# Feed-forward by seven block products, the gated rows through DRAM, the second product as a phase of its own

## The chip, the core and the metric

The kernel runs on one NeuronCore of a Trainium2 chip. The core has a matrix engine (TensorE, "PE" in the rows; its weight loads are "PEld"), a vector engine (VectorE, "DVE"), a scalar engine (ScalarE, "ACT"), GpSimd ("POOL") and SyncE ("SP"), which here issues all DMAs. Each engine works through its own instructions in order; semaphores join them. Operands lie in SBUF (128 partitions); matmuls write to PSUM, eight banks of 128 x 512 float32. The metric is the device time of one execution, in microseconds.

## The reference

Three layers on 1024 tokens of width 1024 (an attention layer with a window, a gated linear attention layer, and a layer with three mixers), with 16 meta tokens ahead of the tokens in the third. The change touches only the feed-forward of that third layer, at the end of the program:

```python
f = causal_dwconv(rms_norm_2(h, norm_ffn_pre) @ ffn_up, ffn_conv)   # 1024 -> 2*2816, 3 taps over tokens
gate, val = jnp.split(f, 2, axis=-1)
f = (jax.nn.gelu(gate, approximate=True) * val) @ ffn_down          # 2816 -> 1024
h = h + rms_norm_2(f, norm_ffn_post)
return h[:, N_META:]
```

Everything is float32. A product of two float32 matrices is made from three matmuls in the type float32r: each operand is split into a high part (a copy in float32r) and a low part (the rest), and high x high, high x low and low x high are summed in PSUM.

## The kernel before

The program is written in a framework that allocates buffers by name ("tag") from pools with a stated number of copies ("bufs"), sets the semaphores itself, and fixes each engine's order of instructions beforehand from a timeline of its own. The order written in the source gives the priority; what is planned as ready earlier can be put ahead. All instructions of the program stand in one straight line, without loops at run time.

`out_proj2` goes through the nine token tiles (16 meta tokens, then 8 x 128). For each it makes the output projection, adds it to the residual, stores the row to DRAM (`hd`), and calls `norm_T` (L290), which normalises the row, transposes it on TensorE in two halves and writes high and low parts of the transposed tokens to `hT3h` and `hT3l` (128 x 8 k x 1040). The caller's `ahead` (L1789) loads and splits the first weights during tiles 3 and 4.

`ffn` goes through 22 blocks of 128 gate and 128 value columns. `block(j)` loads the block's weights of both products and splits them: `wload` (L108) with a copy on ScalarE (L103) and a subtraction on VectorE (L106), four pieces for `ffn_up` ("whi", "wlo"), two for `ffn_down` ("dnh", "dnl"). `up` makes the first product for the two parts in three pieces of 342 tokens each, 24 matmuls a piece (L132 to L134), copies each out of PSUM (L1642), applies the convolution (one scaling on ScalarE, L1644, two multiply-adds on VectorE, L1646), the GELU (L1649) and the gate product (L1650), and splits the gated rows ("fh", "fl"). After every second block `down` makes the second product of the pair for 8 token tiles in two halves of 512 columns, 6 matmuls each, and adds it to an accumulator in SBUF (`acc`, L1662). The first product uses PSUM groups A and E (three banks), the second group B (two banks). In the last pair, `final` closes each token tile: sum of squares (L1670), the post-gain on GpSimd (L1675; VectorE for the last tile), scaling and residual on VectorE (L1676), the store (L1677).

GpSimd has no work in this stage but that of `final` and the reciprocal roots (L97).

## Time and profile before

| | |
|---|---|
| median of 3 runs | 3154.92 us (3152.09 to 3157.61) |
| profiled execution | 3161.62 us, of which the span from first to last instruction is 3159.8 us |
| mean granted TensorE clock | 0.983 of full |
| TensorE busy | 3041.3 us (96%) |
| VectorE, ScalarE, GpSimd busy | 1851.5 (59%), 1400.4 (44%), 463.9 us (15%) |
| feed-forward, first to last matmul | 2395.4 to 3149.4 us |

The rows that follow come from the profile of that one execution. A group row gives the line, engine, operation, the tiles written and read, the shape, the count, then the busy time in us and the mean duration of one in ns, then idle time of the engine ahead of these instructions and what ended it. A row of the timeline gives the start and the duration in us; "x2" joins instructions in a row. Matmuls are pipelined: their recorded durations overlap, so that the distance from start to start says what one costs.

### The profile page before, as it was taken

What the parts mean: (1) busy time and instruction counts of PE and PEld (TensorE: products, weight loads), DVE (VectorE), ACT (ScalarE), POOL (GpSimd) and SP (SyncE); (2) the same over time, 40 slices, a digit from 0 to 9 for tenths busy, and PEclk for the clock granted to TensorE, in tenths of its full rate; (3) what the DMA queues carried; (4) which work ended last, traced back from release to release, by engine and by line L of the source; (5) the groups of instructions that cost most, each with busy time, mean ns of one, the idle gap of its engine ahead of it and who ended that gap; (6) DMA issues with size and microseconds to landing.
All of it is one profiled execution on the core that took longest, in us unless ns stands there. A gap on an engine that the chain in (4) does not pass through costs nothing.

```text
span 3159.8 us, 52021 instructions
## 1 busy us (share of the span) xinstructions
PE 3041.3 (96%) x19891; PEld 2771.9 (88%) x19891; DVE 1851.5 (59%) x4811; ACT 1400.4 (44%) x3415; POOL 463.9 (15%) x506
## 2 busy tenths in 40 slices
PE   8899999999999999998999999899999999999997
PEld 5799999889888789998789999788889999999996
DVE  5667757777766765446547434666555345454446
ACT  4689845555553643323236222345534423233323
POOL 2467621332220000000000000201000000000003
PEclk9999999999999999999999999898999999999999
DMA  5222210110042231113321121313132111111113
GB/s 213 71 75 90 86 40 6 33 34 6 15 144 101 101 101 58 57 39 99 120 77 50 57 70 48 85 46 94 48 123 93 43 40 50 45 47 57 44 40 117
DMA packets 140329, 218.21 MB, mean 69 GB/s; under 512 B 24408, under 2 KB 80784, under 8 KB 140080
## 3 DMA queue, kind: packets, MB, share of 16 engines
q1 hardware_dynamic: 140080, 214.90, 21.6%
q8 instruction: 156, 2.56, 0.3%
q14 instruction: 93, 0.76, 0.1%
HBM read 171.87 MB, written 42.97 MB: 68 GB/s over the span
## 4 chain that ended last, share of the span: by engine, by line
PE 83%; DVE 7%; DMA 4%; ACT 3%; issue 2%; POOL 1%; SPq 0%; DVEq 0%; POOLq 0%; ACTq 0%
PE mm L132 17%; PE mm L133 17%; PE mm L134 17%; PE te L405 3%; PE po L1534 3%; PE sc L391 3%; PE sc L132 2%; PE sc L134 2%; PE sc L133 2%; PE po L661 2%; PE po L612 2%; DMA woraw<-in_w_out 1%; ACT EB L646 1%; PE sc L882 1%; PE tp L255 1%
## 5 line engine op out<-in xcount | busy, mean ns | idle before, releaser
L132 PE MATMUL mm<-whi,hT 128*128 128x256 f32 (+1 forms) x1760 | 513.6, 292 | 19.1 <-DVE gsl L828 4.8
L133 PE MATMUL mm<-wlo,hT 128*128 128x256 f32 (+1 forms) x1760 | 507.2, 289 | 3.5 <-POOL wlo L106 3.5
L132 PEld LDWEIGHTS mm<-whi,hT 128*128 128x128 f32 x1760 | 337.0, 192 | 26.6 <-DVE gsl L828 6.2
L133 PEld LDWEIGHTS mm<-wlo,hT 128*128 128x128 f32 x1760 | 337.5, 192 | 7.3 <-POOL wlo L106 4.8
L132 PE MATMUL mm<-hT3h,whi 128*128 128x342 f32 (+3 forms) x1020 | 325.9, 320 | 0.0
L133 PE MATMUL mm<-hT3l,whi 128*128 128x342 f32 (+3 forms) x1020 | 325.2, 319 | 0.0
L134 PE MATMUL mm<-hT3h,wlo 128*128 128x342 f32 (+3 forms) x1020 | 324.7, 318 | 0.0
L134 PE MATMUL mm<-whi,lo 128*128 128x256 f32 x1040 | 300.7, 290 | 0.9 <-POOL lo L106 0.8
L103 ACT CAST whi<-wraw 128x512 fp32r<-128x512 f32 (+2 forms) x205 | 135.7, 677 | 211.3 <-PE mm L133 79.1
L132 PE MATMUL mm<-hT,whi 128*128 128x352 f32 (+3 forms) x640 | 219.8, 344 | 3.6 <-ACT a L1018 1.8
L1662 DVE TENSOR_TENSOR acc<-acc,sc 128x512 f32<-128x512 f32 x160 | 108.7, 685 | 192.8 <-PE sc L134 192.0
L133 PE MATMUL mm<-hT,whi 128*128 128x352 f32 (+3 forms) x640 | 218.2, 341 | 0.1
L134 PE MATMUL mm<-hT,wlo 128*128 128x352 f32 (+3 forms) x640 | 217.9, 342 | 0.0
L106 DVE TENSOR_TENSOR wlo<-wraw,whi 128x512 fp32r<-128x512 f32 (+1 forms) x161 | 125.9, 789 | 154.1 <-ACT whi L103 153.2
L407 ACT COPY wT<-te 128x512 f32<-128x512 f32 (+2 forms) x368 | 159.3, 453 | 124.1 <-PE te L405 115.8
L134 PE MATMUL mm<-whi,hT 128*128 128x256 f32 (+3 forms) x720 | 205.3, 285 | 0.0
L134 PEld LDWEIGHTS mm<-whi,lo 128*128 128x128 f32 x1040 | 201.8, 194 | 3.1 <-POOL lo L106 1.6
L133 PEld LDWEIGHTS mm<-hT3l,whi 128*128 128x128 f32 x1020 | 192.0, 188 | 6.3
L132 PEld LDWEIGHTS mm<-hT3h,whi 128*128 128x128 f32 x1020 | 191.8, 188 | 6.0
L134 PEld LDWEIGHTS mm<-hT3h,wlo 128*128 128x128 f32 x1020 | 191.9, 188 | 3.6
L97 POOL TENSOR_TENSOR c<-c,cm 128x2 f32<-128x2 f32 (+1 forms) x170 | 126.1, 743 | 404.0 <-DVE c L95 358.1
L97 POOL TENSOR_TENSOR inv<-inv,cm 128x1 f32<-128x1 f32 (+1 forms) x87 | 52.5, 604 | 891.7 <-DVE inv L95 891.7
(490 smaller groups left out, 7687.9 us busy)
## 6 DMA issues: line engine op xcount, KB each, us to landing
adraw<-in_adaln_w SPq DMA_DIRECT2D x48, 512.0 KB, 3.9
wraw<-in_ffn_up SPq DMA_DIRECT2D x85, 256.0 KB, 2.8
wraw<-in_w_ab SPq DMA_DIRECT2D x26, 512.0 KB, 3.8
woraw<-in_w_out SPq DMA_DIRECT2D x48, 256.0 KB, 3.0
wraw<-in_w_gla SPq DMA_DIRECT2D x48, 256.0 KB, 2.9
wraw<-in_w_in SPq DMA_DIRECT2D x24, 512.0 KB, 4.3
dnraw<-in_ffn_down SPq DMA_DIRECT2D x44, 256.0 KB, 2.5
fraw<-qkd SPq DMA_DIRECT2D x32, 260.0 KB, 4.2
```

Source lines behind the costliest of these rows:

```text
L97: nc.gpsimd.tensor_tensor(out, out, self.cm05[:p, :n], op=ALU.pow)
L103: nc.scalar.copy(hi, src)
L106: (lo_eng or nc.vector).tensor_tensor(lo, src, hi.bitcast(F32), op=ALU.subtract)
L132: mmul(ps, ah, bh, start=k == 0, stop=False)
L133: mmul(ps, ah, bl, start=False, stop=False)
L134: mmul(ps, al, bh, start=False, stop=k == nk - 1)
L391: self.nc.tensor.matmul(sp, q[x][:, m], keys, start=x == 0, stop=last and x == 1)
L405: nc.tensor.transpose(ps[:n, j * 128:j * 128 + nq], E, self.ident[:nq, :nq])
L407: nc.scalar.copy(w[:n, :m, :nq], ps.rearrange("p (j t) -> p j t", j=4)[:n, :m, :nq])
L612: nc.tensor.matmul(ops[:, m * 64:m * 64 + 64], w[:, 2 * x + m, :], v[:, i], start=x0 + x + m == 0, stop=x0 + x == len(kt) - 1, skip_group_ ...
L1534: nc.tensor.matmul(ops[:n, :64], w[:kn, y, :n], v[:kn, x, r], start=x == 0, stop=x == i)
L1662: nc.vector.tensor_tensor(acc[:, t, sl], acc[:, t, sl], ps, op=ALU.add)
```

## The change

The matrices of the first product are taken as 2 x 2 blocks: the weights of block j by two halves of the 1024 inner rows and by gate and value columns, the tokens by the same two inner halves and by two halves of the 1024 tokens (514 wide, with two tokens ahead for the convolution). Eight block products give the four results; the change makes them from seven products of sums and differences of blocks (`SEVEN`: weight block, sign, other weight block, token block, sign, other token block).

- `out_proj2` writes the normalised, transposed tokens unsplit into `hf` (128 x 8 x 1026 float32), and splits at once only the two quarters that appear alone in a product (`quads`).
- `tok_op` makes the five other token operands in the first block, when they are first asked for, in two slices of 258 and 256 tokens each (4 x 258 elements a partition) through one buffer `tsum`; products 4 and 6 are summed on GpSimd, 2, 3 and 5 on VectorE; each slice is then split. After block 0 `hf` is freed.
- For each block, `up_raw` loads the weights as two tiles of 512 KB. For each product, `up_op` makes the two half operands (128 x 256): a sum or difference on GpSimd into `uptmp` where there is a sign (five of seven products), then the split. Two pools hold the results, 2 and 9 buffers of each part, and one `uptmp` each.
- For each product and each of two column pieces, 12 matmuls of 258 columns go to one of eight PSUM banks in turn. The first three products are copied to SBUF by ScalarE; VectorE adds the other four out of PSUM, and GpSimd makes the four combinations that lie in SBUF, for each column piece.
- `gate` does convolution, GELU and gate product for a column piece of 256 tokens, gate and value parts as before, and stores the gated rows to DRAM (`fd`, 256 KB).
- The second product follows when all 22 blocks are done (two steps are loaded ahead during block 20): for each half of the tokens and each of the 22 blocks, `step` loads gated rows (256 KB) and `ffn_down` rows (2 x 256 KB), splits them, and 24 matmuls of 512 columns add into all eight banks, which hold the half's result over all 22 blocks. The last three blocks go tile by tile, and `final` works out of the banks, with the post-gain on VectorE.

```diff
@@ out_proj2
-                self.norm_T(h[:n], n, G, None, hT[0], hT[1], c0)
+                xs, m = self.norm_rows(h[:n], n), min(n, 2) if t < 0 else n
                 for half in range(2):
+                    k0, c = 4 * half, max(c0 - 14, 0)
+                    pv = self.half_T(xs, n, half, self.tp).rearrange("p (j t) -> p j t", j=4)[:, :, n - m:n]
+                    dst = hf[:, k0:k0 + 4, c:c + m]
+                    nc.vector.tensor_tensor(dst, pv, G[:, k0:k0 + 4].unsqueeze(2).to_broadcast([128, 4, m]), op=ALU.mult)
+                    x0, x1 = max(c, 512 * half), min(c + m, 514 + 512 * half)
+                    if x0 < x1:
+                        q = slice(x0 - 512 * half, x1 - 512 * half)
+                        self.split(*(z[:, :, q] for z in quads[half]), hf[:, k0:k0 + 4, x0:x1],
+                                   "dve" if half == 0 else "act")
@@ ffn, with the functions removed (they stand above) left out
+    SEVEN = [((1, 0), 1, (1, 1), (0, 0), 0, None),
+             ((0, 0), 1, (0, 1), (1, 1), 0, None),
+             ((0, 0), 1, (1, 1), (0, 0), 1, (1, 1)),
+             ((1, 1), 0, None, (1, 0), -1, (0, 0)),
+             ((0, 0), 0, None, (0, 1), -1, (1, 1)),
+             ((1, 0), -1, (0, 0), (0, 0), 1, (0, 1)),
+             ((0, 1), -1, (1, 1), (1, 0), 1, (1, 1))]
+    def up_raw(self, j, pool):
+        raws = []
+        for q in range(2):
+            raw = pool.tile([128, 2, 2, 256], F32, tag="upraw", name="upraw", bufs=2)
+            self.nc.sync.dma_start(raw, self.I["ffn_up"][j].rearrange("p (h q i) c -> q p h i c", h=2, q=2)[q])
+            raws.append(raw)
+        return raws
+    def up_op(self, raws, i, pools):
+        nc = self.nc
+        (r, h), sign, other = self.SEVEN[i][:3]
+        parts = []
+        for raw in raws:
+            pool, bufs = next(pools)
+            src = raw[:, h, :, 128 * r:128 * r + 128]
+            if sign:
+                r2, h2 = other
+                tmp = pool.tile([128, 2, 128], F32, tag="uptmp", name="uptmp", bufs=1)
+                nc.gpsimd.tensor_tensor(tmp, src, raw[:, h2, :, 128 * r2:128 * r2 + 128],
+                                        op=ALU.add if sign > 0 else ALU.subtract)
+                src = tmp
+            p = [pool.tile([128, 2, 128], F32R, tag="up" + z, name="up" + z, bufs=bufs) for z in "hl"]
+            self.split(*p, src)
+            parts.append(p)
+        return lambda k: tuple(z[:, k % 2] for z in parts[k // 2])
+    def ffn(self, hd, hf, close_hf, quads, wp, early, out):
+        nc, I = self.nc, self.I
+        st = ExitStack()
+        sp = st.enter_context(self.pool("hS", 1))
+        w1 = st.enter_context(self.pool("wtsu", 1))
+        p = st.enter_context(self.pool("ffn", 2))
+        cw = p.tile([128, 3, 44], F32, name="ffnc", bufs=1)
+        nc.sync.dma_start(cw, I["ffn_conv"])
+        fd = [self.dp.tile([128, 2, 512], F32, name=f"fd{j}") for j in range(22)]
+        self.psum(mm="ABDCABDE")
+        pools = itertools.cycle([(wp, 2)] + [(w1, 9)] * 4 + [(wp, 2)] + [(w1, 9)] * 5)
+        halves = [slice(0, 512), slice(512, 1024)]
+        sums = {}
+        def tok_op(i):
+            qa, sign, qb = self.SEVEN[i][3:]
+            if not sign:
+                return quads[qa[0]]
+            if i not in sums:
+                a, b = (hf[:, 4 * r:4 * r + 4, 512 * h:512 * h + 514] for r, h in (qa, qb))
+                op = [sp.tile([128, 4, 514], F32R, name=f"s{i}{z}") for z in "hl"]
+                for c in (slice(0, 258), slice(258, 514)):
+                    s = (slice(None), slice(None), c)
+                    t = sp.tile([128, 4, 258], F32, tag="tsum", name="tsum")[:, :, :c.stop - c.start]
+                    (nc.gpsimd if i in (4, 6) else nc.vector).tensor_tensor(
+                        t, a[s], b[s], op=ALU.add if sign > 0 else ALU.subtract)
+                    self.split(op[0][s], op[1][s], t)
+                sums[i] = op
+            return sums[i]
+        def block(j, raws, first):
+            x = [[p.tile([128, 2, 258], F32, tag=f"fx{part}", name="fx") for part in range(2)] for c in range(2)]
+            s = [[None] * 7 for c in range(2)]
+            for i in range(7):
+                w = first if first and i == 0 else self.up_op(raws, i, pools)
+                op = tok_op(i)
+                for c in range(2):
+                    ps = self.mm()[:, :258]
+                    for k in range(4):
+                        wh, wl = w(k)
+                        th, tl = (z[:, k, 256 * c:256 * c + 258] for z in op)
+                        nc.tensor.matmul(ps, wh, th, start=k == 0, stop=False)
+                        nc.tensor.matmul(ps, wh, tl, start=False, stop=False)
+                        nc.tensor.matmul(ps, wl, th, start=False, stop=k == 3)
+                    g, u = x[c]
+                    if i < 3:
+                        s[c][i] = p.tile([128, 258], F32, tag=f"fs{i}", name=f"fs{i}")
+                        nc.scalar.copy(s[c][i], ps)
+                    s0, s1, s2 = s[c][:3]
+                    if i == 2:
+                        nc.gpsimd.tensor_tensor(s2, s2, s0, op=ALU.subtract)
+                        nc.gpsimd.tensor_tensor(s2, s2, s1, op=ALU.subtract)
+                    elif i == 3:
+                        nc.vector.tensor_tensor(u[:, 0], ps, s0, op=ALU.add)
+                        nc.gpsimd.tensor_tensor(s0, s2, u[:, 0], op=ALU.add)
+                    elif i == 4:
+                        nc.vector.tensor_tensor(g[:, 1], ps, s1, op=ALU.add)
+                        nc.gpsimd.tensor_tensor(s1, s2, g[:, 1], op=ALU.add)
+                    elif i == 5:
+                        nc.vector.tensor_tensor(u[:, 1], ps, s1, op=ALU.add)
+                    elif i == 6:
+                        nc.vector.tensor_tensor(g[:, 0], ps, s0, op=ALU.add)
+                        self.gate(p, cw, j, x[c], fd[j][:, :, 256 * c:256 * c + 256])
+        def step(h, k):
+            pool, n = ((P, 2), (P, 2), (Q, 4), (Q, 4), (Q, 4), (Q, 4))[(22 * h + k) % 6] if h + k > 1 else (P, 2)
+            fr = pool.tile([128, 512], F32, tag="fr", name="fr", bufs=2)
+            nc.sync.dma_start(fr, fd[k][:, h])
+            f = [pool.tile([128, 512], F32R, tag="f" + z, name="f" + z, bufs=n) for z in "hl"]
+            self.split(*f, fr)
+            d = [pool.tile([128, 1024], F32R, tag="dn" + z, name="dn" + z, bufs=n) for z in "hl"]
+            for sl in halves:
+                raw = pool.tile([128, 512], F32, tag="dnraw", name="dnraw", bufs=2)
+                nc.sync.dma_start(raw, I["ffn_down"][k][:, sl])
+                self.split(*(z[:, sl] for z in d), raw)
+            return f, d
+        with ExitStack() as s2:
+            for j in range(22):
+                if j:
+                    raws, w0 = self.up_raw(j, wp), None
+                block(j, raws, w0)
+                if j == 0:
+                    close_hf()
+                    P = s2.enter_context(self.pool("dn1", 1, side="right"))
+                if j == 20:
+                    ready = [step(0, 0), step(0, 1)]
+            st.close()
+            Q = s2.enter_context(self.pool("dn2", 1))
+            post = Q.tile([128, 1024], F32, name="npost2")
+            nc.sync.dma_start(post, I["norm_ffn_post"].partition_broadcast(128))
+            self.psum(dn="AABBCDDE")
+            LAST = 3
...
+            for h in range(2):
+                banks = [[self.bank("dn") for i in range(2)] for t in range(4)]
+                def mm(t, i, k, f, d):
+                    a, b = ([z[:, s] for z in q] for q, s in ((f, slice(128 * t, 128 * t + 128)), (d, halves[i])))
+                    for n, (e, g) in enumerate(((0, 0), (0, 1), (1, 0))):
+                        nc.tensor.matmul(banks[t][i], a[e], b[g], start=k == 0 and n == 0, stop=k == 21 and n == 2)
+                for k in range(22 - LAST):
+                    f, d = ready.pop(0) if ready else step(h, k)
+                    for t in range(4):
+                        for i in range(2):
+                            mm(t, i, k, f, d)
+                last = [step(h, k) for k in range(22 - LAST, 22)]
+                for t in range(4):
+                    for i in range(2):
+                        for k in range(LAST):
+                            mm(t, i, 22 - LAST + k, *last[k])
+                    final(4 * h + t, banks[t])
+    def gate(self, p, cw, j, x, dst):
+        nc = self.nc
+        ys = []
+        for part in range(2):
+            y = p.tile([128, 2, 256], F32, tag=f"fy{part}", name="fy")
+            c = 22 * part + j
+            nc.scalar.activation(y, x[part][:, :, 2:258], AF.Copy, scale=cw[:, 2, c:c + 1])
+            for tap in range(2):
+                nc.vector.scalar_tensor_tensor(y, x[part][:, :, tap:tap + 256], cw[:, tap, c:c + 1], y, op0=ALU.mult,
+                                               op1=ALU.add)
+            ys.append(y)
+        g, u = ys
+        nc.scalar.activation(g, g, AF.Gelu_apprx_tanh)
+        nc.vector.tensor_tensor(g, g, u, op=ALU.mult)
+        nc.sync.dma_start(dst, g)
```

## Rows read from the trace of the kernel before

**Rows 1.** The page's part 4: who holds the chain that ended last.
```profile
PE 83%; DVE 7%; DMA 4%; ACT 3%; issue 2%; POOL 1%; SPq 0%; DVEq 0%; POOLq 0%; ACTq 0%
```

**Rows 2.** Three stretches: us, busy PE, PEld, DVE, ACT, POOL, clock, DMA.
```profile
2395.40:2450.00 54.60, 53.31 (x341) 52.53 (x340) 32.85 (x42) 28.59 (x47) 1.41 (x2) 1.00 0.33 108
2450.00:3095.00 645.00, 645.00 (x3656) 602.59 (x3655) 304.99 (x363) 203.67 (x316) 0.00 (x0) 1.00 0.15 46
3095.00:3149.60 54.60, 48.64 (x246) 39.97 (x244) 39.91 (x66) 20.79 (x50) 22.03 (x20) 0.97 0.36 121
```

**Rows 3.** Timeline, TensorE: first and last of 31, 32, 12 matmuls.
```profile
2449.79 0.32 PE L132 MATMUL mm<-hT3h,whi 128*128 128x342 f32 x1
...
2454.48 0.32 PE L132 MATMUL mm<-hT3h,whi 128*128 128x342 f32 x1
...
1299.72 0.28 PE L132 MATMUL mm<-whi,hT 128*128 128x256 f32 x1
...
1303.44 0.28 PE L133 MATMUL mm<-wlo,hT 128*128 128x256 f32 x1
...
2460.39 0.39 PE L132 MATMUL sc<-dnh,fh 128*128 128x512 f32 x1
...
2462.95 0.39 PE L134 MATMUL sc<-dnh,fl 128*128 128x512 f32 x1
```

**Rows 4.** VectorE: two groups by shape, then three rows of its timeline.
```profile
L106 DVE TENSOR_TENSOR qTl<-tp,qTh 128x256 fp32r<-128x256 f32 x80 | 33.5, 419 | 12.9 <-ACT qTh L103 12.0
L106 DVE TENSOR_TENSOR wlo<-wraw,whi 128x1024 fp32r<-128x1024 f32 x26 | 32.9, 1266 | 41.8 <-ACT whi L103 41.7
...
3096.32 0.75 DVE L1646 SCALAR_TENSOR_TENSOR fy<-fx,ffnc,fy 128x510 f32<-128x510 f32 x1 [2.31 <-ACT fy L1644]
...
3108.15 0.69 DVE L1650 TENSOR_TENSOR fy<-fy 128x510 f32<-128x510 f32 x1
...
3110.82 1.28 DVE L106 TENSOR_TENSOR dnl<-dnraw,dnh 128x512 fp32r<-128x512 f32 x2
```

**Rows 5.** ScalarE, groups by shape: a cast, a scaling, a wide cast.
```profile
L103 ACT CAST fh<-fy 128x256 fp32r<-128x256 f32 x1 | 0.4, 391 | 0.0
L1644 ACT ACTIVATE fy<-fx,ffnc 128x510 f32<-128x510 f32 x2 | 1.4, 724 | 0.1
L103 ACT CAST whi<-wraw 128x1024 fp32r<-128x1024 f32 x26 | 27.2, 1046 | 73.7 <-PE mm L133 36.3 <-DMA wraw<-in_w_in 20.4 <-DMA wraw<-in_w_ab 14.9
```

**Rows 6.** GpSimd, groups by shape: sums over SBUF in an earlier layer.
```profile
L182 POOL TENSOR_TENSOR adacc<-adacc,adpr 128x512 f32<-128x512 f32 x84 | 107.9, 1285 | 37.4 <-ACT adpr L179 25.9 <-ACT adacc L179 6.8 <-PE sc L391 1.9
L182 POOL TENSOR_TENSOR adacc<-adacc,adpr 128x256 f32<-128x256 f32 x28 | 20.7, 740 | 10.6 <-ACT adpr L179 6.7 <-ACT adacc L179 2.5
```

**Rows 7.** One VectorE line (durations min/median/max), then two pairs beside GpSimd.
```profile
L365 DVE TENSOR_TENSOR qn<-jk,jk x64: 404/424/1524, 72.1 to 878.0; 128x256 f32<-128x256 f32 x64
...
210.89 2.65 POOL L182 TENSOR_TENSOR adacc<-adacc,adpr 128x512 f32<-128x512 f32 x2 [0.47 <-ACT adpr L179]
...
212.36 1.47 DVE L365 TENSOR_TENSOR qn<-jk,jk 128x256 f32<-128x256 f32 x1
...
3133.05 2.96 POOL L1675 TENSOR_TENSOR acc<-acc,npost 128x512 f32<-128x512 f32 x2
...
3133.11 3.45 DVE L1676 SCALAR_TENSOR_TENSOR acc<-acc,inv,h 128x512 f32<-128x512 f32 x2
```

**Rows 8.** Timeline: last output-projection matmul, and the last token tile's low part.
```profile
2394.82 0.39 PE L134 MATMUL mm<-wo 128*128 128x512 f32 x1
...
2408.69 0.69 DVE L106 TENSOR_TENSOR hT3l<-xt,hT3h 128x512 fp32r<-128x512 f32 x1
```

**Rows 9.** Timeline: the last matmul, and VectorE's last two instructions.
```profile
3149.00 0.40 PE L134 MATMUL sc<-dnh,fl 128*128 128x512 f32 x1
...
3155.40 1.41 DVE L1676 SCALAR_TENSOR_TENSOR acc<-acc,inv,h 128x512 f32<-128x512 f32 x2 [0.73 <-POOL inv L97]
```

**Rows 10.** DMA issues: times, KB each, median us from issue to landing.
```profile
adraw<-in_adaln_w SPq DMA_DIRECT2D x48, 512.0 KB, 3.9
```

More of the change, by code (lines that the diff above doesn't have):

```diff
@@ new lines, in ffn, with final @@
+    def ffn(self, hd, hf, close_hf, quads, wp, early, out):
[59 more added lines that the diff above has]
+                        self.gate(p, cw, j, x[c], fd[j][:, :, 256 * c:256 * c + 256])
+        raws, w0 = early
+        P = None
+        steps = []
+        def step(h, k):
[26 more added lines that the diff above has]
+            LAST = 3
+            def final(t, banks):
+                h = Q.tile([128, 1024], F32, tag="h", name="h", bufs=2)
@@ L1666, in final @@
                 nc.sync.dma_start(h, hd[t + 1])
+                y = Q.tile([128, 1024], F32, tag="y", name="y", bufs=2)
                 ss, rs = self.sums()
@@ L1669, in final @@
                 for i, sl in enumerate(halves):
-                    nc.scalar.activation(self.te(), acc[:, t, sl], AF.Square, accum_out=ss[:, i:i + 1])
+                    jk = Q.tile([128, 512], F32, tag="jk", name="jk", bufs=2)
+                    nc.scalar.activation(jk, banks[i], AF.Square, accum_out=ss[:, i:i + 1])
+                    nc.vector.tensor_tensor(y[:, sl], banks[i], post[:, sl], op=ALU.mult)
                 nc.vector.tensor_tensor(rs, ss[:, 0:1], ss[:, 1:2], op=ALU.add)
@@ L1673, in final @@
                 for i, sl in enumerate(halves):
-                    y = acc[:, t, sl]
-                    (nc.gpsimd if t < 7 else nc.vector).tensor_tensor(y, y, post[i], op=ALU.mult)
-                    nc.vector.scalar_tensor_tensor(y, y, rs, h[:, sl], op0=ALU.mult, op1=ALU.add)
-                    nc.sync.dma_start(out[t * 128:t * 128 + 128, sl], y)
-            for g in range(10):
-                Bs = []
-                for j in (2 * g, 2 * g + 1):
-                    Bs.append(block(j))
-                    up(Bs[-1], FC)
-                for t in range(8):
-                    down(Bs, t, g == 0)
@@ L1687, in ffn @@
-            Bs = [block(20)]
-            up(Bs[0], FC)
-            Bs.append(block(21))
-            post = []
-            for sl in halves:
-                post.append(self.wp.tile([128, 512], F32, tag="wraw", name="npost2", bufs=RAWS))
-                nc.sync.dma_start(post[-1], I["norm_ffn_post"][sl].partition_broadcast(128))
-            FC = [(14, 512), (526, 258), (784, 256)]
-            up(Bs[1], FC[:1])
-            up(Bs[1], FC[1:2])
-            for ts, nxt in ((range(0, 3), FC[2:]), (range(3, 6), None), (range(6, 8), None)):
-                for t in ts:
-                    down(Bs, t, False)
-                    final(t)
-                if nxt:
-                    up(Bs[1], nxt)
+                    nc.vector.scalar_tensor_tensor(y[:, sl], y[:, sl], rs, h[:, sl], op0=ALU.mult, op1=ALU.add)
@@ new lines, in final @@
+                    nc.sync.dma_start(out[t * 128:t * 128 + 128, sl], y[:, sl])
+            for h in range(2):
[15 more added lines that the diff above has]
+                    final(4 * h + t, banks[t])
@@ L1784, in build @@
             hp = st.enter_context(self.pool("hT3", 1, side="right"))
-            hT = [hp.tile([128, 8, 1040], F32R, name="hT3" + s) for s in "hl"]
+            quads = [[hp.tile([128, 4, 514], F32R, name=f"q{q}{z}") for z in "hl"] for q in range(2)]
             wp, early = st.enter_context(self.pool("wts3", 1, side="right")), []
+            hfs = ExitStack()
+            hf = hfs.enter_context(self.pool("hf", 1, side="right")).tile([128, 8, 1026], F32, name="hf")
             def ahead(t):
-                for x in {3: (0, 1), 4: (2,)}.get(t, ()):
-                    raw = oin2.tile([128, 2, 256], F32, tag="x", name="upraw")
-                    nc.sync.dma_start(raw, I["ffn_up"][0][:, 2 * x:2 * x + 2])
-                    early.append([wp.tile([128, 2, 256], F32R, name=f"up{z}{x}") for z in "hl"])
-                    self.split(*early[-1], raw)
-            self.out_proj2(wo2, oin2, o2, lod, hd, gp[:, 1], hT, ahead)
+                if t == 3:
+                    raws = self.up_raw(0, wp)
+                    early.extend((raws, self.up_op(raws, 0, itertools.repeat((wp, 2)))))
+            self.out_proj2(wo2, oin2, o2, lod, hd, gp[:, 1], hf, quads, ahead)
             wos.close()
-            self.ffn(hd, hT, early, out)
+            self.ffn(hd, hf, hfs.close, quads, wp, early, out)
 @with_exitstack
```

56 lines of the change are left out of this document (1 added, 55 removed).

## Prediction

> **What bounds the kernel now.** I read the chain that ended last first: TensorE holds 83% of it, VectorE 7% [rows 1]. Then the busy time by stretch [rows 2]: from 2450 to 3095 us, the body of the feed-forward, TensorE has no idle time at the full clock, while VectorE is busy 305 of 645 us, ScalarE 204 and GpSimd not at all. What the matmuls of this stage cost is therefore worth its full price, and whatever the change adds on the other engines is free only until one of them gets as long as TensorE. The price of a matmul is its spacing, not its recorded duration (records overlap): 30 steps of 342 columns take 4.69 us, 0.1563 each; 11 steps of 512 columns 2.56 us, 0.2327; 31 steps of 256 columns 3.72 us, 0.1200 [rows 3]. Between 256 and 342 columns that is 0.42 ns a column, so 0.1208 us for 258 columns, interpolated between two rows.
>
> **First product.** Before: 22 blocks x 2 parts x 3 pieces x 8 k x 3 = 3168 matmuls of 342 columns, 495.2 us, 22.5 a block. After: 22 x 7 products x 2 column pieces x 4 k x 3 = 3696 matmuls of 258 columns, 446.5 us, 20.3 a block. TensorE alone gains **48.7 us**: 12% of the columns go, but there are 528 more instructions, and each carries about 13 ns beyond its columns.
>
> What a block now asks of the others. VectorE: 14 low parts of 128x256 at 0.42 (5.9 us), 8 sums out of PSUM at about the same 0.42 (3.4), 8 taps of 512 at 0.75 (6.0), 2 gate products at 0.69 (1.4): 16.6 us; two instructions in a row took 1.28 where 0.69 stands for one, so back to back each is some 0.09 cheaper, 32 x 0.09 = 2.9, about 13.8 us [rows 4]. ScalarE: 14 high parts and 6 PSUM copies at 0.39, 4 scalings at 0.72, 2 GELUs at no more than that: 12 us [rows 5]. GpSimd, idle here before: 10 weight sums and 8 sums of products at 0.74: 13.3 us [rows 6]. Each fits into 20.3 us by itself.
>
> They do not run by themselves. When a GpSimd sum over SBUF is under way, a VectorE instruction with both operands in SBUF waits until it ends: a 128x256 product whose median is 0.424 us took 1.47, beginning inside a pair of GpSimd sums (210.89 to 213.54) and ending 0.29 after them; two 512 products, 0.75 each, took 3.45 beside two GpSimd products [rows 7]. The first ended 0.29 us behind GpSimd's end though it needs 0.42, so VectorE is let in about 0.12 before that end, and a 0.74 sum shuts it out for about 0.62. Of a block's 32 VectorE instructions 24 have both operands in SBUF (13.3 us); the 8 PSUM sums have one. If the two never overlapped, a block would take 13.3 + 13.3 = 26.6 us; if they never met, TensorE's 20.3. Between these ends I take the row: 13.8 us of VectorE, plus 18 shut-outs of up to 0.62, of which a quarter fall on PSUM sums and a part on VectorE's own idle time and instruction starts; at 0.35 to 0.4 each that is 6.3 to 7.2, together 20 to 21 us. That is TensorE's own length. There is a second chain of that length: the buffer "uptmp" of a weight sum is single in its pool (9 of 11 half operands use the same pool), so sum 0.74, copy 0.39, subtraction 0.42 and the hand-overs follow each other, 1.7 to 2.3 us for each of about 8.2 a block (14 to 19 us), and the two raw tiles of the next block can load only when the last product's sums have read the present ones, 3.9 us to land [rows 10]. Five and a half operands of lead (11 buffers) hide that load while the lead lasts. Three limits within 5% of each other, in an order fixed beforehand, add something to the longest: I take **21.4 us a block**, 1.1 over TensorE's, 22 x 1.1 = **+24 us** (ends 0 and 22 x 6.3 = +139).
>
> The Trainium skill, page "SBUF — State Buffer", section "Who interferes with whom", speaks against this change: it says that a VectorE instruction with two SBUF inputs and a GpSimd instruction reading SBUF exclude each other for a whole instruction, and that one with at most one SBUF input does not contend. The rows above agree, but for the 0.12. By whole instructions the sum would be the upper end, 26.6 us a block and some 3250 us; by the rows it is the 21.4.
>
> **First block.** The last output-projection matmul of the stage ahead begins at 2394.82 and the last token tile's low part at 2408.69; before, chunks of earlier tokens fill that time, and 53.31 of the first 54.6 us are busy [rows 2, 8]. After, product 0 needs the first tokens alone, product 1 the last ones, and products 2 to 6 need sums that are made once, ten slices of about 1032 elements through one buffer. Six are summed on VectorE (1.27), four on GpSimd (2 x 1.29), then a copy (1.05) and a subtraction (1.27) [rows 4 to 6]: 6 x 3.6 + 4 x 4.9 = 41 us one after another. TensorE has 20.3 us of this block to do, so up to 41 - 20.3 and the late start, some 30 us, are open; slices that are ready early, and products 0 to 2 of the next block, fill a part. I take **+18** (5 to 32).
>
> **Second product.** 1056 matmuls of 512 columns as before: **0**. A step (24 matmuls, 5.6 us) asks 3 casts and 3 subtractions of 512, about 2 us on each engine, no GpSimd, and 768 KB: 137 GB/s; with six steps of buffers I hide that. If loads came late, each 0.1 us a step costs 4.4 (range -5 to +8). The change of phase needs the banks emptied and the area of the first phase freed; two steps, 11 us, are loaded ahead: **+3** (0 to 8). The 44 stores of gated rows and 44 loads back ride on SP's queue; 160 additions into "acc" leave VectorE, off the path.
>
> **End.** From 3095 us TensorE idles 6 us behind the closing sums and GpSimd products, at a clock of 0.97 [rows 2]; the last matmul begins at 3149.00, and VectorE is still at work at 3155.40 [rows 9], in a span of 3159.8. After, nothing interrupts TensorE here, the post-gain is applied straight from the banks, and 5 to 6 us follow the last matmul instead of 10.4: **-11** (-6 to -13).
>
> **Sum.** -48.7 + 24 + 18 + 0 + 3 - 11 = -14.7 us. The profiled execution took 3161.6 (span 3159.8), so 3146.9; the median of the runs is 3154.92, 6.7 lower, so 3140.
>
> **Rivals.** (a) TensorE paces: the lead absorbs every shut-out, 20.3 us a block, and the next block fills more of the first, +12: -48.7 + 12 + 3 - 11 = -45, **3110**. For it: VectorE, ScalarE and GpSimd each need under 17 us, and 8 banks decouple TensorE from late sums. Against: rows 7. (b) The shared port decides: the other terms make -38.7, so from 22 x 1.76, that is **22.1 us a block**, the change loses. At 24, midway between my value and the upper end: -48.7 + 81 + 18 + 3 - 11 = +42, **3197**. For it: at the end of the kernel, the one place of this stage with GpSimd products, VectorE is where TensorE waits (53.31 of 54.6 us busy at the start, 48.64 here) [rows 2, 7]; the single uptmp buffer lets each shut-out add to a chain. Against: there only two banks took the sums, here eight. (c) The change does not do what it says because SP's queue has the raw loads of a block behind the gated-row stores of the block before: then the lead is lost, and gate (about 4 us), load (3.9) and first operand (1.6) stand between blocks, 22 x 9.5 = +209, about 3350. Against: the buffers are free some 13 us earlier, and the planner issues what is ready.
>
> **How the numbers follow.** My forecast, 20.8 to 22.1 us a block, 3127 to 3155, has a chance of 0.40 (0.32 faster, 0.06 the same, 0.02 slower); (a) 0.22, all faster; (b) 0.32 (0.05 the same, 0.27 slower); (c) 0.06, slower. Faster by over 0.2% (6.3 us, about what a measurement of this kernel can tell from no change): 0.54; the same 0.11; slower 0.35. The range leaves out the lowest quarter of (a), all of (c) and what of (b) lies over 24.8 us a block: 3098 to 3215. The forecast's own range is its 3127 to 3155.
>
> **What would show it.** Spacing of 258-column matmuls at 0.120 to 0.121 us. Start to start of blocks 20.3 (a), 21 to 22 (mine), 23 and more (b), with VectorE durations of taps and low parts above 0.75 and 0.42 by the shut-outs and TensorE waiting for "upl" written by VectorE. Ten "tsum" slices in a row until about 2445 us. In the second phase 5.5 to 5.6 us a step without idle time; 5 to 6 us behind the last matmul. The forecast is wrong if GpSimd's sums turn out hidden wholly, if the first block waits under 5 us or over 32, or if the second phase waits for loads.

## The result, and the profile after

The changed kernel took 3209.45 us in the median of four runs (3206.19 to 3216.22), the kernel before 3156.27 beside it: a ratio of 1.0167 (95% interval 1.0137 to 1.0196), **1.7% slower**. The forecast was 3140, faster; the time lies inside the range, near its upper end. The profiled execution of the changed kernel took 3207.53 us, with a span of 3205.6.

The chain that ended last (part 4 of the page), shares by engine:

```profile
PE 71%; DVE 12%; ACT 5%; POOL 5%; DMA 4%; issue 3%; SPq 0%; DVEq 0%; POOLq 0%; ACTq 0%
```

The busy time by stretch, columns as in [rows 2]: blocks 0 to 2, blocks 3 to 21, the second product, and a window of 350 us that the experiments below share.

```profile
2391.20:2496.90 105.70, 81.54 (x524) 75.30 (x523) 86.10 (x121) 48.17 (x99) 62.66 (x59) 0.81 0.21 66
2496.90:2957.60 460.70, 418.09 (x3188) 400.45 (x3187) 328.23 (x608) 206.34 (x491) 278.26 (x340) 0.96 0.20 68
...
2957.60:3198.30 240.70, 240.70 (x1059) 198.08 (x1057) 105.77 (x177) 83.37 (x160) 3.86 (x7) 1.00 0.50 163
...
2500.00:2850.00 350.00, 317.69 (x2423) 304.14 (x2424) 249.05 (x463) 158.57 (x381) 211.56 (x259) 0.97 0.20 67
```

TensorE's share of the chain has fallen from 83% [rows 1] to 71%. Where it had no idle time in the body of the stage [rows 2], it now waits in the whole first product and makes 2423 matmuls in 350 us, a block of 168 in 24.3 us. The second product has no gap.

The waits of GpSimd in the same 350 us (us in total, times, longest):

```profile
POOL uptmp L1648 <- DVE upl L106: 128.2, 85, 3.6
POOL fs L1709 <- ACT fs L1706: 7.0, 9, 0.9
POOL uptmp L1648 <- DMA upraw<-in_ffn_up: 4.7, 8, 2.5
```

Three groups of VectorE in the same window, columns as in [rows 4]:

```profile
L1803 DVE SCALAR_TENSOR_TENSOR fy<-fx,ffnc,fy 128x512 f32<-128x512 f32 x115 | 101.0, 905 | 7.0 <-ACT fy L1801 6.7
L106 DVE TENSOR_TENSOR upl<-uptmp,uph 128x256 fp32r<-128x256 f32 x146 | 68.0, 467 | 54.5 <-ACT uph L103 54.1
L1712 DVE TENSOR_TENSOR fx<-mm,fs 128x258 f32<-128x258 f32 x29 | 12.3, 425 | 16.3 <-PE mm L1702 15.9
```

GpSimd works 211.6 of the 350 us; its waits of the three rows add up to 139.9 (one reaches over the window's edge), nine tenths of them for a subtraction on VectorE that reads an "uptmp" buffer. Two effects are visible at once. GpSimd waits for its buffer, and VectorE's instructions with two operands in SBUF are longer than in the rows of before: the taps 0.905 us against 0.75, the low parts 0.467 against 0.419 [rows 4]. The sums out of PSUM stay at 0.425.

One link of the chain, from the timeline of the three engines (start, duration):

```profile
2667.45 1.88 DVE L1803 SCALAR_TENSOR_TENSOR fy<-fx,ffnc,fy 128x512 f32<-128x512 f32 x2
...
2667.61 1.17 POOL L1648 TENSOR_TENSOR uptmp<-upraw 128x256 f32<-128x256 f32 x1 [0.36 <-DVE upl L106]
2668.81 0.41 ACT L103 CAST uph<-uptmp 128x256 fp32r<-128x256 f32 x1 [0.50 <-POOL uptmp L1648]
2669.25 0.41 DVE L106 TENSOR_TENSOR upl<-uptmp,uph 128x256 fp32r<-128x256 f32 x1
...
2669.74 1.19 POOL L1648 TENSOR_TENSOR uptmp<-upraw 128x256 f32<-128x256 f32 x1 [0.96 <-DVE upl L106]
```

Sum, cast, low part, next sum: 2.13 us, of which the sum takes 1.17 instead of 0.74 [rows 6] with two taps on VectorE beside it, and those take 1.88 for two.

This link is shorter than the mean. Of the 146 weight sums in the window, matched in order with their casts and low parts, 46 begin before the low part of the sum ahead is done, so these two lie in the buffers of different pools. 60 begin right behind that low part, 2.61 us after the sum ahead in the mean: 0.98 for the sum, 0.41 for the cast, 0.42 for the low part, and 0.80 of hand-overs, 0.54 of it while the low part waits its turn on VectorE.

**The balance** of the two spans (3205.6 - 3159.8 = +45.8): the last output-projection matmul begins 3.9 us earlier (2390.89 against 2394.82 [rows 8]); the first product's matmuls at TensorE's own pace, 20.05 us a block as the experiments show it, are 441.1 instead of 495.2, -54.1; TensorE waits or runs at half clock in the first product for 566.4 - 441.1 = +125.3 us, 45.5 of it in blocks 0 to 2 and 79.8 in blocks 3 to 21; the second product is 5.0 shorter; 13.3 us of idle time of before are gone (2394.82 to 3149.00 is 754.2, the matmuls 740.9); the end is 3.4 shorter. Together +45.6.

### The profile page after: what moved, and what is told of

Read it like the earlier page. It is cut to its first block, busy times and chain, and to the rows that moved or that the text cites. A ratio compares the mean times of both kernels' runs of the same rounds, so it can differ in the third digit from the quotient of the medians.

```text
span 3205.6 us, 54674 instructions
## 1 busy us (share of the span) xinstructions
PE 3034.4 (95%) x20419; PEld 2749.9 (86%) x20419; DVE 1986.4 (62%) x5238; ACT 1478.8 (46%) x3740; POOL 786.2 (25%) x892
## 3 DMA queue, kind: packets, MB, share of 16 engines
q1 hardware_dynamic: 163872, 249.50, 24.3%
## 4 chain that ended last, share of the span: by engine, by line
PE 71%; DVE 12%; ACT 5%; POOL 5%; DMA 4%; issue 3%; SPq 0%; DVEq 0%; POOLq 0%; ACTq 0%
PE mm L132 12%; PE mm L133 12%; PE mm L134 12%; PE dn L1780 8%; DVE fy L1803 3%; PE te L405 3%; PE po L1534 3%; PE sc L391 3%; DVE upl L106 2%; PE po L661 2%; POOL uptmp L1648 2%; PE po L612 2%; PE mm L1702 1%; PE mm L1700 1%; PE mm L1701 1%
## 5 line engine op out<-in xcount | busy, mean ns | idle before, releaser
L1648 POOL TENSOR_TENSOR uptmp<-upraw 128x256 f32<-128x256 f32 x220 | 199.2, 908 | 287.4 <-DVE upl L106 196.2
L1803 DVE SCALAR_TENSOR_TENSOR fy<-fx,ffnc,fy 128x512 f32<-128x512 f32 x176 | 152.9, 895 | 11.3 <-ACT fy L1801 10.9
L103 ACT CAST uph<-uptmp 128x256 fp32r<-128x256 f32 x220 | 88.9, 405 | 152.2 <-POOL uptmp L1648 148.0
L106 DVE TENSOR_TENSOR upl<-uptmp,uph 128x256 fp32r<-128x256 f32 x220 | 110.6, 505 | 76.3 <-ACT uph L103 75.6
L397 DVE TENSOR_SCALAR_CACHE_REDUCE EB<-sc 128x512 f32<-128x512 f32 (+1 forms) x208 | 120.0, 584 | 35.9 <-PE sc L391 33.2
L182 POOL TENSOR_TENSOR adacc<-adacc,adpr 128x512 f32<-128x512 f32 (+1 forms) x112 | 129.0, 1152 | 47.9 <-ACT adpr L179 32.8
L103 ACT CAST whi<-wraw 128x512 fp32r<-128x512 f32 (+2 forms) x120 | 84.1, 719 | 118.4 <-PE mm L133 45.4
L391 PE MATMUL sc<-kT,qTh 128*128 128x256 f32 (+2 forms) x352 | 125.5, 371 | 13.3 <-DVE EB L397 6.6
L134 PEld LDWEIGHTS mm<-whi,hT 128*128 128x128 f32 (+1 forms) x720 | 136.5, 190 | 1.5
## 6 DMA issues: line engine op xcount, KB each, us to landing
adraw<-in_adaln_w SPq DMA_DIRECT2D x48, 512.0 KB, 3.8
upraw<-in_ffn_up SPq DMA_DIRECT2D x44, 512.0 KB, 3.7
wraw<-in_w_ab SPq DMA_DIRECT2D x26, 512.0 KB, 3.7
wraw<-in_w_in SPq DMA_DIRECT2D x24, 512.0 KB, 4.2
```

Source lines behind the costliest of these rows:

```text
L103: nc.scalar.copy(hi, src)
L106: (lo_eng or nc.vector).tensor_tensor(lo, src, hi.bitcast(F32), op=ALU.subtract)
L134: mmul(ps, al, bh, start=False, stop=k == nk - 1)
L182: nc.gpsimd.tensor_tensor(a, a, pr[:, :conds], op=ALU.add)
L391: self.nc.tensor.matmul(sp, q[x][:, m], keys, start=x == 0, stop=last and x == 1)
L1648: nc.gpsimd.tensor_tensor(tmp, src, raw[:, h2, :, 128 * r2:128 * r2 + 128], op=ALU.add if sign > 0 else ALU.subtract)
```

## The experiments

Four suspects for the 125 us: T1, GpSimd and VectorE shut each other out; T2, one buffer for a weight sum makes a chain; T3, the raw tiles are one block deep; T4, the product sums stand in GpSimd's queue ahead of the next block's weight sums. The comparisons go by "first product", first to last of its matmuls in the profile (566.4 us in the changed kernel), and by the 350 us window.

**Two buffers.**

```diff
-tmp = pool.tile([128, 2, 128], F32, tag="uptmp", name="uptmp", bufs=1)
+tmp = pool.tile([128, 2, 128], F32, tag="uptmp", name="uptmp", bufs=1 if bufs == 2 else 2)
-pools = itertools.cycle([(wp, 2)] + [(w1, 9)] * 4 + [(wp, 2)] + [(w1, 9)] * 5)
+pools = itertools.cycle([(wp, 2)] + [(w1, 8)] * 4 + [(wp, 2)] + [(w1, 8)] * 4)
```

> The changed kernel with two buffers for the tile of a weight sum in the resident pool instead of one (and one buffer fewer for the converted results: 8 in place of 9). Nothing else changes. Changed kernel: 3209 us, a steady block 24.2 us. Theory T1 (shared access: GpSimd's 18 sums a block and VectorE's 24 operations with two operands in SBUF shut each other out, so the sum of both paces the block): nothing moves, 3200 to 3215 us, block 24 us. Theory T2 (the single buffer makes a chain sum, conversion, subtraction, next sum of 2.4 us a link, ten links a block): the chain opens, the block falls to between 20.3 us (TensorE's pace) and 22 us, 3122 to 3160 us.

3152.51 us, a ratio to the kernel before of 0.998 (0.997 to 0.9989): 57 us gone by one buffer of 1 KB a partition. First product 511.2. T2 holds, and T1 alone can't be the cause.

**Four raw tiles**, in a pool of their own.

```diff
-raw = pool.tile([128, 2, 2, 256], F32, tag="upraw", name="upraw", bufs=2)
+raw = pool.tile([128, 2, 2, 256], F32, tag="upraw", name="upraw", bufs=4)
```

> The changed kernel with four raw weight tiles (two blocks) instead of two, in a pool of their own from block 1 to block 19. Nothing else changes. Theory T3 (the raw tiles are one block deep, so the next block's loads wait for this block's last weight sums, and GpSimd starts each block late): the weight sums run ahead into the next block and the block falls by 1 to 2 us, 3165 to 3190 us. T1 (shared access of GpSimd and VectorE) and T2 (chain through one sum buffer): nothing moves, 3200 to 3215 us.

3210.19 us (1.0172, 1.0146 to 1.0198), first product 566.9. T3 falls for the changed kernel; the raw loads ended only 4.7 us of GpSimd's waits to begin with.

**GpSimd without shared reads.**

```diff
-nc.gpsimd.tensor_tensor(tmp, src, raw[:, h2, :, 128 * r2:128 * r2 + 128], op=...)
+for z in range(2):
+    nc.gpsimd.memset(tmp, float(z))
+nc.gpsimd.tensor_copy(tmp[:, :, :1], raw[:, h2, :, 128 * r2:128 * r2 + 1])
-nc.gpsimd.tensor_tensor(s0, s2, u[:, 0], op=ALU.add)      # and the three others on fs
+[nc.gpsimd.memset(s0, float(z)) for z in range(2)]
```

> The changed kernel with every GpSimd sum in the first product (ten weight sums and eight product sums a block) replaced by two fills of the same tile with a constant, which read nothing; the weight sums keep a tiny copy of two columns after the fills, so that they still wait for the raw load. This part of the computation is left out (the sums are not formed). GpSimd is as long busy as with the sum alone, by estimate: a fill of 128x512 took 0.53 us in the trace, so two fills of 128x256 take 0.6 to 0.8 us, the sum alone 0.74. T1 (shared access): with no second reader VectorE's operations return to 0.42 and 0.75 us, the block goes to TensorE's 20.3 us, 3110 to 3135 us. T2 and T3 (chain through one sum buffer, raw tiles one block deep): GpSimd's own time and the order are the same, so the time stays at 3190 to 3215 us.

3168.18 us (1.0033, 1.0018 to 1.0048), between the two answers: first product 523.9. So T1 costs something, though not all. The fills are not quite as long as sums that run alone: GpSimd works 12.8 us a block here, 14.7 in the changed kernel, and 13.3 was its price alone. Up to 0.5 us a block of the gain may be that. **Both edits together**, two buffers and fills:

> Both earlier edits: two buffers for the tile of a weight sum, and all GpSimd sums of the first product replaced by two fills each (a tiny copy keeps the wait for the raw load). The sums are left out of the computation. With two buffers alone the steady block took 21.1 us (the later ones 21.8), with fills alone 22.6 us. Theory T1 for the rest (with the chain open, what is left above TensorE's 20.3 us is the shared access of GpSimd and VectorE): 20.3 to 20.5 us a block, 3122 to 3140 us. If the rest is VectorE's own work or the raw loads: 21 to 21.8 us a block, 3146 to 3158 us.

3115.41 us (0.9861, 0.9839 to 0.9884), first product 470.9. The window of 350 us with two buffers alone:

```profile
2500.00:2850.00 350.00, 335.85 (x2713) 328.38 (x2711) 294.64 (x515) 167.10 (x414) 253.98 (x289) 1.00 0.22 75
```

With fills alone:

```profile
2500.00:2850.00 350.00, 327.33 (x2612) 316.30 (x2612) 227.66 (x492) 166.70 (x402) 198.58 (x721) 1.00 0.22 73
```

With both:

```profile
2500.00:2850.00 350.00, 350.00 (x2932) 350.00 (x2931) 252.01 (x555) 184.18 (x448) 209.57 (x808) 1.00 0.25 79
```

The low parts in that window in the changed kernel (durations min/median/max in ns):

```profile
L106 DVE TENSOR_TENSOR upl<-uptmp,uph x146: 406/417/1041, 2499.7 to 2848.6; 128x256 fp32r<-128x256 f32 x146
```

And with fills alone:

```profile
L106 DVE TENSOR_TENSOR upl<-uptmp,uph x154: 410/420/427, 2501.2 to 2847.0; 128x256 fp32r<-128x256 f32 x154
```

With both edits TensorE has no idle time and makes 2932 matmuls, 20.05 us a block: its own pace. With fills alone no low part is longer than 0.427 us, though the copies of two columns still read SBUF, and the chain still holds the block at 22.5. The four first products make a square:

| first product, us | GpSimd sums | GpSimd fills |
|---|---|---|
| one buffer | 566.4 | 523.9 |
| two buffers | 511.2 | 470.9 |

The second buffer gives 55.2 and 53.0, the end of the shared reads 42.5 and 40.3: two costs that add, near enough without interaction, and together all that lies above TensorE's pace but the start (29.8). That fits the Trainium skill, page "SBUF — State Buffer", section "Who interferes with whom": VectorE with two SBUF inputs contends with a GpSimd instruction that reads SBUF, not with one that only writes. The trace agrees by the 0.427 us.

**Product sums on VectorE**, with one weight-sum buffer as in the changed kernel.

```diff
-nc.gpsimd.tensor_tensor(s0, s2, u[:, 0], op=ALU.add)      # and the three others on fs
+nc.vector.tensor_tensor(s0, s2, u[:, 0], op=ALU.add)
```

> The changed kernel with the eight product sums a block (on fs) on VectorE; the ten weight sums stay on GpSimd. T1 (shared access): operations with two SBUF operands are then 32 on VectorE (13.3 + 8 x 0.42 = 16.7 us) and 10 on GpSimd (7.4 us); added up less some 2 us of overlap at their edges that is 22.1 us a block, 3160 us (3145 to 3180). T4 (the product sums stand in GpSimd's queue ahead of the next block's weight sums, and this order costs the time): GpSimd's queue is free for the weight sums, the block comes to TensorE's 20.3 us or VectorE's 16.8 + 3.4 = 20.2 us, 3120 to 3140 us. T2 alone (ten links of the chain, 2.4 us each): 24 us, no change.

3169.55 us (1.0036, 1.002 to 1.0053), 22.6 us a block. T1's number, but with the single buffer still in place the chain could give it too; T4 as the main cause falls.

**Token sums in quarters**, through two buffers of half the size and all on VectorE, on top of the second weight-sum buffer.

```diff
-t = sp.tile([128, 4, 258], F32, tag="tsum", name="tsum")[:, :, :c.stop - c.start]
-(nc.gpsimd if i in (4, 6) else nc.vector).tensor_tensor(
+t = sp.tile([128, 4, 129], F32, tag="tsum", name="tsum", bufs=2)[:, :, :c.stop - c.start]
+nc.vector.tensor_tensor(
```

> Two buffers for the tile of a weight sum, and the token sums of block 0 in quarters instead of halves, in two buffers of half the size instead of one, all on VectorE (before that four of the ten on GpSimd). With two buffers for the weight sums alone the first three blocks take 97 us, 36 us above TensorE's 20.3 each. If the loss there is the chain sum, conversion, subtraction, next sum through one buffer and GpSimd's sums of 2.4 us: it falls by 10 to 15 us, 3136 to 3144 us. If VectorE's work (25 us for the ten sums and their subtractions) or the low clock of TensorE after the last output projection sets it: no change, 3148 to 3157 us.

3148.28 us (0.9972, 0.996 to 0.9984). The median is 4 us below that of two buffers alone and the intervals overlap: the gain is not 10 to 15 us, and whether there is any stays open. VectorE was busy for 102 of the first 109 us.

**The product sums out of PSUM.** The difference of products can be taken while they lie in a bank:

```diff
-nc.gpsimd.tensor_tensor(s2, s2, s0, op=ALU.subtract)
-nc.gpsimd.tensor_tensor(s2, s2, s1, op=ALU.subtract)
+nc.vector.tensor_tensor(s[c][2], ps, s1, op=ALU.subtract)
+nc.vector.tensor_tensor(s[c][3], ps, s0, op=ALU.subtract)
...
-nc.gpsimd.tensor_tensor(s0, s2, u[:, 0], op=ALU.add)
+nc.vector.tensor_tensor(s2, ps, s2, op=ALU.add)
...
-nc.gpsimd.tensor_tensor(s1, s2, g[:, 1], op=ALU.add)
+nc.vector.tensor_tensor(s3, ps, s3, op=ALU.add)
```

> Two buffers for the tile of a weight sum and the token sums in quarters on VectorE, as in the run before, and no product sum on GpSimd: the third product's bank is read twice by VectorE (less the second product, less the first), and the fourth and fifth bank are each added to these, so that the eight product sums a block become eight more VectorE operations that read PSUM and one tile in SBUF. In the changed kernel such operations took 0.42 us beside GpSimd, as alone, while those with two operands in SBUF grew from 0.75 to 0.90 and from 0.42 to 0.47. T1 (only operations with two operands in SBUF are shut out): VectorE 16.8 + 8 x 0.42 = 20.2 us a block, the shared operations 13.3 + 10 x 0.74 = 20.7 less 2 at the edges, so both near TensorE's 20.05: 20.1 to 21 us a block, 3112 to 3135 us. If what counts is VectorE's own work and its waits together: over 21.5 us a block, 3145 to 3160 us.

**3117.12 us, 0.9877 (0.9858 to 0.9897): 1.2% faster than the kernel before.** First product 472.6. The window of 350 us:

```profile
2500.00:2850.00 350.00, 349.02 (x2905) 348.61 (x2905) 330.61 (x703) 174.10 (x420) 147.79 (x177) 1.00 0.24 81
```

Two groups of VectorE in it, a sum as before and a new one, both out of PSUM:

```profile
L1720 DVE TENSOR_TENSOR fx<-mm,fs 128x258 f32<-128x258 f32 x36 | 14.9, 415 | 0.0
L1718 DVE TENSOR_TENSOR fs<-mm,fs 128x258 f32<-128x258 f32 x36 | 14.8, 410 | 0.0
```

VectorE works 331 of 350 us, more than in any other run, and TensorE is idle for 1. How much VectorE does was not what counted. The edit takes two things away at once, the shared reads of the eight sums and their place in GpSimd's queue (15.7 us of GpSimd's work a block with two buffers alone, 8.5 here), and no run separates them in this version. In the run with two buffers and fills GpSimd's queue kept all its places, 12.0 us a block, and the first product was as short (470.9), so in that run the end of the shared reads was enough. The same page and section of the Trainium skill say that a VectorE instruction with at most one SBUF input, outside the 2-port perf modes, does not contend with GpSimd. The 0.41 us here agree.

This version also has the second weight-sum buffer and the token sums in quarters. **The same with one weight-sum buffer again**:

```diff
-name="uptmp", bufs=1 if bufs == 2 else 2)
+name="uptmp", bufs=1)
```

> The same kernel, with the token sums, but one buffer for the tile of a weight sum as in the changed kernel. T2 (a link sum, conversion, subtraction, next sum): ten links at 0.87 + 0.40 + 0.53 us and three hand-overs of 0.1 to 0.2 us, 2.2 us a link, 22 us a block where TensorE takes 20.15: 3150 to 3160 us. If the buffer mattered only because GpSimd also had the product sums: no change, 3112 to 3122 us.

3150.86 us (0.9964, 0.9951 to 0.9977), first product 512.0: the second buffer gives 39 us of the first product here too, 34 in the medians. The window:

```profile
2500.00:2850.00 350.00, 338.49 (x2694) 331.43 (x2693) 309.71 (x639) 160.79 (x383) 134.37 (x160) 0.98 0.22 73
```

GpSimd does nothing but weight sums now, and its waits in the window show the chain, and the raw loads beside it:

```profile
POOL uptmp L1648 <- DVE upl L106: 171.4, 123, 3.0
POOL uptmp L1648 <- DMA upraw<-in_ffn_up: 42.1, 21, 4.1
```

160 sums in 350 us are one in 2.19 us, 21.9 us for the ten of a block. That is the block's pace divided by ten, and not the length of a link: 75 of the sums begin before the low part of the sum ahead is done, 64 begin right behind it, 2.35 us after the sum ahead, and 42 us, 2.6 a block, go to waits for raw loads, which were 4.7 us in the changed kernel. Whether more raw tiles would help in this version was not tried.

**The version with two buffers and PSUM sums, without token sums**:

```diff
-if not sign:
-    return quads[qa[0]]
+return quads[qa[0]]
```

> The run before (two sum buffers, no product sum on GpSimd) without the token sums of block 0: each product takes one of the two plain quarters in their place, so this part of the computation is left out; matmuls, weight sums and everything after are the same in number and size. With the token sums the first three blocks took 87.5 us, 27 above TensorE's 20.15 each, and the time was 3117 us. If the token sums (20 sums, conversions and subtractions, most on VectorE, which was busy 103 of the first 109 us) make this loss: 20 to 27 us less, 3090 to 3097 us. If the wait for the last norm and TensorE's low clock make it: 0 to 8 us less, 3109 to 3117 us.

3102.84 us in two runs (0.9817, 0.9786 to 0.9849), between the answers. The first product falls by 19.7 us to 452.9, so most of the start's loss (31.5) is the token sums; but the second product grows from 240.6 to 248.0: TensorE waits 4.5 us at its third step for ScalarE's cast of the loaded rows, and runs at the lower clock for a while behind it (0.65 over the next 8.2 us). The next run has the same stop and shows where it comes from.

**The second product alone**: the first product of before, its gated rows to DRAM, then the changed kernel's second phase.

```diff
-self.split(B.f[0][:, a:b], B.f[1][:, a:b], g)
+nc.sync.dma_start(fd[j], g.rearrange("p (h t) -> p h t", h=2))
```

> The second part of the change alone: the first product as in the kernel before (eight block products a block, pieces of 342 columns, raw weights converted without sums, no GpSimd), but its gated rows go to DRAM, and the second product is the changed kernel's own phase in all banks, with its end. Price from the trace of the changed kernel: second product at 0.227 us a matmul in place of 0.2327, 1056 of them, so 6 us less; from its last matmul to the end of the program 7.4 us in place of 10.8, and the idle of TensorE among the last tiles gone, together about 10 us less; the change of phase 0.1 us. If the first product of seven block products is what costs the time: 16 us below the kernel before, 3138 to 3150 us. If the passage through DRAM or the missing accumulation beside the matmuls costs as much as it gives: within 0.2% of the kernel before, 3153 to 3165 us.

3146.59 us (0.9969, 0.9958 to 0.998). So this part is worth 10.7 us, and the seven block products as they were written cost 63 more than this version (their first product is 566.4 against 497.9 us; 9 of these 68 are lost again here at the change of phase). Of the 16 us forecast 5 are missing, and the change of phase takes them: the second product lasts 249.8 us instead of 240.6; the timeline of TensorE there:

```profile
2897.92 0.39 PE L1691 MATMUL dn<-dnh,fl 128*128 128x512 f32 x1
2905.28 2.07 PE L1691 MATMUL dn<-dnh,fh 128*128 128x512 f32 x4 [6.97 <-ACT dnh L103]
```

The windows around it:

```profile
2898.00:2905.30 7.30, 0.33 (x3) 0.02 (x1) 2.81 (x5) 3.15 (x6) 0.00 (x0) 0.89 0.92 309
2905.30:2912.00 6.70, 6.70 (x19) 5.31 (x20) 2.25 (x4) 2.09 (x4) 0.00 (x0) 0.61 0.90 352
```

TensorE stops for 7 us because the third step isn't loaded, and for the next 7 us its granted clock is 0.61 in the mean. SP's queue shows why: the last store of gated rows, then the third step's first load:

```profile
2893.02 0.32 SPq L1637 DMA_DIRECT2D fd<-fy  x1
...
2897.06 0.42 SPq L1646 DMA_DIRECT2D fr<-fd  x1
```

In the version with two buffers and PSUM sums the two stand the other way round, the load first:

```profile
2858.56 0.45 SPq L1733 DMA_DIRECT2D fr<-fd  x1
...
2871.04 0.52 SPq L1811 DMA_DIRECT2D fd<-fy  x1
```

SP works through its queue in order, and a store waits for the gate's result (22.2 us here). Behind the last store the third step's load is issued 9.8 us after the second product has begun (2887.26), when the two steps loaded ahead are nearly used up, and it lands late, with the DMA engines 92% busy; ahead of that store, it was issued 7.8 us before it began (2866.35). The version without token sums has the order of this run, 8.0 us after the start; the changed kernel and all its other versions have the load ahead. The order is fixed beforehand by the framework, and no run changed it alone.

## Why the prediction was wrong, point by point

- **Matmuls**: right. 258 columns were priced at 0.1208 us; 168 in 20.05 us are 0.1193. The gain at TensorE's pace is 54 us rather than 48.7.
- **The steady block**: the step that failed. It was taken as 21.4 us and measured 24.3 (a mean of 24.25 over blocks 3 to 21); 54 of the 78 us that the first product took beyond the forecast are here. Three limits (VectorE with its shut-outs, the chain, TensorE) were set side by side, and a little was put on the longest. VectorE's was priced too high: 20 to 21 us against 17.3 of work a block (14.6 with fills, so the shut-outs lengthen VectorE by 2.7 us, not by 6.3 to 7.2). The chain's was priced too low, at 8.2 links of 1.7 to 2.3 us, 14 to 19 us a block. The number of links fits the trace, in which the other pool's sums run beside the chain; their length does not: 2.61 us where one sum follows directly on another, an estimate of 21.4 us for 8.2 of them, over TensorE's pace. The hand-overs, above all the low part's turn on VectorE, and the sum stretched from 0.74 to 0.98 us were the undersized parts. And limits that work on each other don't leave only the longest: the square shows the two costs adding, 2.4 to 2.5 us a block for the single buffer and 1.8 to 1.9 for the shared reads.
- **Rival (b)** gave 24 us a block and 3197 us, close to what came, by the shared port. The number was right and the reason no more than half: with two buffers, the port in place, the block is 21.7. That the single buffer lets shut-outs add to a chain stood there as a remark, without a price of its own.
- **First block**: +18 forecast, 5 to 32 allowed, also too low. Measured from the first product's start, blocks 0 to 2 lose 45.5 us in the changed kernel, about 12.6 of that at the steady rate, so some 33. About 10 of the 45.5 are matmuls 0.215 us apart, at the lower clock (granted 0.81 over these blocks). The slices ran in one chain until about 2450, near the 2445 forecast; that the following blocks could fill less than assumed, since their weight sums need the same engines, is likely but not shown.
- **The clock**: no step for it. In blocks 3 to 21 the granted clock is 0.96, and it was 1.00 in this stage before. TensorE pauses often there, and nine times, behind one or more pauses whose longest was 0.9 to 2.2 us, the clock is at its lower level of 1.2 GHz for a stretch. The first such stretch has pauses of 0.55, 0.68 and 0.90 us ahead of it, and the granted clock is 0.57 from 2503.7 to 2507.5; in the timeline, a pause and two matmuls behind it, 0.21 us apart:

```profile
2503.75 0.39 PE L1702 MATMUL mm<-q1h,upl 128*128 128x258 f32 x1 [0.90 <-DVE upl L106]
...
2506.19 0.42 PE L1701 MATMUL mm<-q1l,uph 128*128 128x258 f32 x1
2506.40 0.42 PE L1702 MATMUL mm<-q1h,upl 128*128 128x258 f32 x1
```

  The waits are paid a second time so: 188 matmuls about 0.215 us apart cost 18.6 us over their price at the full clock, inside the 79.8. With two buffers, or with fills, the granted clock in the window is 1.00, although TensorE still idles 14 and 23 of the 350 us.
- **Second product** (0, measured -5.0), **change of phase** (+3, measured 0.1) and **end** (-11 against the idle time and the tail of before): the end has 7.4 us behind the last matmul instead of 5 to 6, and the 6 us of idle time are gone, so about -9. The spacing is 0.227 instead of 0.2327. The change of phase cost nothing here because the third step's loads stand ahead of the last stores in SP's queue; where they stand behind them, it costs 9 and 7 us (249.8 and 248.0 instead of 240.6). A faster first product alone does not bring that on: at 472.6 and 470.9 us the second product still took 240.6.
- **Rival (c)**, SP's queue: no sign of it between the blocks; four raw tiles changed nothing. Loads held up behind stores of gated rows, its mechanism, came only at the change of phase of two other versions. **Rival (a)**, TensorE's pace, is what the version with two buffers and PSUM sums reaches: 3117 against the 3110 worked out for it.
- **The direction**: the break-even stood at 22.1 us a block. The single buffer without shared reads holds the block at 22.5, the shared reads without the single buffer at 21.7, and both together at 24.3. With 2.6 us a link and the two costs added, a slower kernel would have been the forecast.

## What to carry to other kernels

A helper buffer with one copy ties three in-order engines into a chain: count its links for the whole loop body, price each with the time that its instructions wait their turn on the other engines (here 0.8 of 2.6 us), and compare links x link time with the bound engine before asking about contention; here a second copy of 1 KB a partition was worth 57 us. When GpSimd is given sums over SBUF, look for the ones that could read PSUM instead: eight product sums moved to VectorE, the busier engine, made the kernel 31 us faster. Where one stage's stores and the next stage's loads share a queue, look at their order in the trace of every version: here nearly the same source gave a stop of 4.5 us or none.

## What the runs showed of the hardware that was not expected

- A GpSimd fill of 128x256 takes 0.313 us, one of 128x512 0.533 elsewhere in the changed kernel, and a copy of two columns of 128 partitions 0.281: the fill's time grows with its size, and a copy of two columns costs nearly as much as a fill of 256.
- A VectorE operation on one PSUM and one SBUF operand keeps 0.41 to 0.43 us beside GpSimd sums, at any load that these runs made; low parts, with two SBUF operands, reached 1.04 us.
- Nine times in blocks 3 to 21 the granted clock fell to its lower level behind pauses of TensorE whose longest was 0.9 to 2.2 us; behind 7 us without work in the run of the second product alone, 512-column matmuls stood 0.427 us apart from 2905.28 to 2910.5.
